# A hybrid streaming encoder: top-k masks taken from ScalarE's signs, and a convolution's input kept as one row

## The chip, the cores and the metric

The kernel runs on 1 core of one Trainium2 chip. The metric is the device time of one execution in microseconds (us); before the change it is 2071.84 us, the median of 3 runs (2068.47 to 2072.87). Engines are named as in the profile: PE (matmul), PEld (its weight loads), DVE (VectorE), ACT (ScalarE), POOL (GpSimd) and SP (which issues the DMAs).

## The reference, cut to what matters

The program is one inference step of a two-layer encoder, for 1024 prompt tokens and 64 sample tokens (1088 in all). Each layer normalises x, projects it with one combined matrix `w_in` to 5204 columns, and feeds three branches: A, a causal convolution of width 4 and a gated linear recurrence; B, sparse attention; C, a causal convolution of width 4, SiLU and a chunked state-space scan (SSD). Their outputs are concatenated, projected by `w_out` and added to x. The parts that the change touches are these:

```python
def causal_conv(x, buf, w, b):              # CONV_WIDTH = 4, buf holds the last 3 tokens
    xp = jnp.concatenate([buf, x], axis=1)
    y = b
    for j in range(CONV_WIDTH):
        y = y + xp[:, j:j + T] * w[j]
    return y, xp[:, T:]

# in sparse_attention, for each block of 64 query tokens
score = sum_h w[t,h] * relu(q_idx[t,h] . k_idx[s])
score = jnp.where(admissible, score, -jnp.inf)
_, idx = lax.top_k(score, k_top)            # k_top = min(256, keys // 4)
# ... attention runs over the chosen keys alone
```

`top_k` takes the highest scores and, among equal ones, those that stand first.

## The kernel before, in words

**Layout.** Channels stand on partitions and tokens along the free axis, in three chunks of 384, 384 and 320 tokens. A projection of one block of 128 columns (`projection`, `three`) takes, for each chunk, 24 matmuls: 8 row tiles of h, three products each (L215 to L217), because both operands are split into a high and a low part. The result lies in one of three PSUM banks named `mm` until ACT or DVE has evacuated it; transposes and small products use two banks named `tp`. A chunk's matmuls therefore wait for the evacuation of the chunk three before.

**Selection.** For seven tiles j of query tokens (score rows `sc` of 384, 512, ... 1024 and 576 keys; six of 128 rows, the last of 64) `select` finds each row's threshold by a binary search over the bits of a float: 31 steps, four tiles counted by ACT with Sign and an accumulator (L580), three by DVE (L574). Before the search the scores are multiplied by a sign `sg` (+1 or -1 per row) so that the threshold sought is never negative (`flip`, L583). After it a mask is made for each tile: the scores are flipped back (L583), DVE counts those at or below the threshold (L574, `le`), marks those equal to it (L631, `eq`), numbers the equal ones by a scan (L634, into `sc`, which is not needed any more), keeps those that stand beyond the number that is wanted (L633, L636, L637), and multiplies by 2^100 (L638). The mask (0 chosen, 2^100 not) goes into `shared`. `select` is a generator: one search step or one mask per `yield`; `pace()` takes one step after each projection, at a lower priority, and what is left runs after `steps(g[0])`.

**Convolution.** `conv_project` projects a block and lets `evac` write each chunk into a tile `raw` of 387 columns: 3 columns of history and 384 of data. The history of chunks 1 and 2 is copied by DVE from the tile of the chunk before (L831); chunk 0's is set to 0 (L833). In chunk 2 the sample's 3 history columns come from the state (L838) between the prompt's and the sample's tokens, and two copies keep the new state (L841, L842). There are 3 buffers of `raw`, one per chunk. `conv4` reads four shifted views of `raw`: one on ACT (L849), with `spare` a second one on ACT and POOL (L852, L853), the others on DVE (L855). Twelve blocks of branch C (`xbc`) run in the stretch of the search, four of branch A (`lru`) after the masks.

**What sets the order.** The order on each engine is fixed when the program is built: a scheduler takes the operations by priority, in about the order of the code, and places them by a simulated timeline; `PLAN` is the list of blocks (`x`, `X` a convolution block of branch C, `z` and `a` gates, `q` a query block, `s` a step of the SSD scan, `l` and `g` branch A). When the chip runs, each engine takes its own instructions strictly in that order. Near the masks stand in the code: the last `x` blocks, then `a0 q1 q0 a1`. A gate (L411 on ACT, L412 on DVE) and a query block (`normed`: transposes L652 on PE, squares L657 on ACT, products L658 on DVE) need DVE to free their PSUM banks.

## Time and profile before

| | |
|---|---|
| median of 3 runs | 2071.84 us |
| profiled execution | 2070.2 us, of which the span from first to last instruction is 2068.4 us |
| PE busy | 1962.7 us (95%) |
| PEld busy | 1755.5 us (85%) |
| DVE busy | 1530.1 us (74%) |
| ACT busy | 1206.6 us (58%) |
| POOL busy | 648.1 us (31%) |
| mean granted TensorE clock | 0.975 |

Read it by stages, not as a whole. Layer 0 fills the time to about 1030 us, layer 1 the rest, with the same stages: normalisation and scores, then (150 to 400 us) projections beside the threshold search, then (400 to 475 us) the masks, then branch A and the second half of SSD (to 675 us), attention and the output projection. An engine that is busy 58% over the span may be idle in the one stage that matters, or bound it. Matmuls are pipelined: their count in a window says more than their busy time. A wait is put down to the instruction that came last.

### The profile page before, as it was taken

The page shows a single profiled execution, that of the slowest core. Times are in us where ns is not written, and L with a number is a line of the kernel's source. Part 1 is how long each engine was busy: PE and PEld are TensorE (multiplying, and loading weights), DVE is VectorE, ACT ScalarE, POOL GpSimd, SP SyncE. Part 2 cuts the span into 40 slices and gives each one's busy share as a digit, 9 for nine tenths or more (in the row PEclk, how much of TensorE's full clock was granted, in tenths as well). Part 3 has the DMA queues.
Part 4 walks back from the last instruction along what each step waited for, and adds up shares of the span by engine and source line. Part 5 has one row for each costly group of instructions (what it writes and reads, how often), then busy time and mean ns, then how long its engine had stood idle before and what let it go on. Part 6 is the DMA issues. An engine that isn't in the chain of part 4 may idle for free.

```text
span 2068.4 us, 34696 instructions
## 1 busy us (share of the span) xinstructions
PE 1962.7 (95%) x12056; PEld 1755.5 (85%) x12056; DVE 1530.1 (74%) x3805; ACT 1206.6 (58%) x2525; POOL 648.1 (31%) x561
## 2 busy tenths in 40 slices
PE   6999999899899899999999999998999998999999
PEld 5899989888789787866998998998888887877689
DVE  7778999997867855564387889999976868456723
ACT  6579898624655544454355798985256655444521
POOL 3012244323522422243430222444243314223320
PEclk9999999999999899999999999999999998999999
DMA  6124354526433632324541433545254246224145
GB/s 225 62 78 135 99 172 130 165 77 164 118 105 108 205 111 87 109 81 128 193 135 38 120 128 105 152 140 162 68 162 113 93 149 194 91 96 141 42 137 173
DMA packets 252080, 257.95 MB, mean 125 GB/s; under 512 B 31264, under 2 KB 230304, under 8 KB 251904
## 3 DMA queue, kind: packets, MB, share of 16 engines
q1 hardware_dynamic: 251904, 255.73, 40.3%
q8 instruction: 95, 1.56, 0.3%
q14 instruction: 81, 0.66, 0.1%
HBM read 181.09 MB, written 74.57 MB: 124 GB/s over the span
## 4 chain that ended last, share of the span: by engine, by line
PE 60%; DVE 20%; DMA 9%; ACT 6%; issue 4%; SPq 1%; POOL 1%; DVEq 0%; ACTq 0%; POOLq 0%
PE mm L215 14%; PE mm L216 14%; PE mm L217 14%; PE s L1098 4%; PE tp L1093 3%; PE s L1068 3%; DMA cumB<-cumd 2%; ACT junka L580 2%; DVE u L855 1%; PE s L881 1%; DVE junk L574 1%; PE s L514 1%; ACT cumB L739 1%; DVE cumB L741 1%; DMA xsc<-xsd 1%
## 5 line engine op out<-in xcount | busy, mean ns | idle before, releaser
L193 POOL TENSOR_TENSOR wlo<-wraw,whi 128x1024 fp32r<-128x1024 f32 x80 | 197.8, 2472 | 361.4 <-ACT whi L192 361.1
L580 ACT ACTIVATE junka<-sc,cand 128x768 bf16<-128x768 f32 x248 | 239.3, 968 | 9.9 <-DVE cand L600 5.7
L192 ACT ACTIVATE whi<-wraw 128x1024 fp32r<-128x1024 f32 x130 | 137.0, 1054 | 136.2 <-PE mm L216 82.6
L1075 ACT ACTIVATE lg<-lg,mx 128x512 f32<-128x512 f32 (+8 forms) x144 | 111.1, 772 | 105.4 <-DVE mx L1071 105.1
L1095 ACT ACTIVATE pT<-tp 128x512 f32<-128x512 f32 (+1 forms) x164 | 90.0, 567 | 114.9 <-PE tp L1093 113.5
L1060 POOL TENSOR_TENSOR nbm<-nb,shared 128x256 f32<-128x256 f32 (+1 forms) x112 | 80.9, 727 | 242.2 <-DVE mx L1071 219.7
L855 DVE SCALAR_TENSOR_TENSOR u<-raw,parh,u 128x384 f32<-128x384 f32 (+1 forms) x198 | 134.7, 689 | 8.9 <-POOL u L853 4.5
L574 DVE TENSOR_SCALAR_CACHE_REDUCE junk<-sc,cand 128x384 bf16<-128x384 f32 (+4 forms) x194 | 140.0, 753 | 0.9
L1068 PE MATMUL s<-kst,qst 128*128 128x512 f32 (+4 forms) x448 | 119.3, 363 | 10.5 <-DVE mx L1071 10.5
L739 ACT ACTIVATE cumB<-cumB,ctk 128x128 f32<-128x128 f32 (+1 forms) x288 | 88.4, 384 | 51.4 <-DMA cumB<-cumd 51.1
L1093 PEld LDWEIGHTS tp<-identr,lg 128*128 128x128 f32 (+2 forms) x656 | 71.5, 140 | 48.7 <-issue 42.2
L1093 PE MATMUL tp<-identr,lg 128*128 128x128 f32 (+2 forms) x656 | 108.5, 278 | 0.5 <-DVE lg L1078 0.5
L1098 PE MATMUL s<-pT,vt 128*64 128x256 f32 (+2 forms) x656 | 106.8, 391 | 1.6 <-ACT pT L1095 1.6
L215 PE MATMUL mm<-sth0a,whi 128*128 128x384 f32 (+1 forms) x228 | 84.2, 370 | 16.9 <-DVE g L412 11.2
L1071 DVE CUSTOM_DVE_ANT_0 lg<-s,shared 128x512 f32<-128x512 f32 (+4 forms) x112 | 61.5, 553 | 46.7 <-PE s L1068 41.7
L1068 PEld LDWEIGHTS s<-kst,qst 128*128 128x128 f32 (+1 forms) x448 | 72.3, 188 | 25.4 <-DVE mx L1071 16.7
L1078 DVE TENSOR_SCALAR lg<-lg,ri 128x512 f32<-128x512 f32 (+8 forms) x144 | 87.1, 607 | 3.2
L1143 DVE TENSOR_TENSOR xl<-xl,mm 128x384 f32<-128x384 f32 (+1 forms) x40 | 21.4, 540 | 90.1 <-PE mm L217 71.3
L216 PE MATMUL mm<-stl0a,whi 128*128 128x384 f32 (+1 forms) x228 | 80.0, 351 | 2.1 <-POOL stl0a L954 1.6
L193 DVE TENSOR_TENSOR wlo<-wraw,whi 128x1024 fp32r<-128x1024 f32 x50 | 63.6, 1271 | 23.9 <-ACT whi L192 23.6
L216 PE MATMUL mm<-stl1a,whi 128*128 128x384 f32 (+1 forms) x228 | 80.2, 352 | 1.0 <-DVE stl1a L954 0.8
L217 PE MATMUL mm<-sth3a,wlo 128*128 128x384 f32 (+1 forms) x228 | 80.5, 353 | 0.0
(474 smaller groups left out, 6915.9 us busy)
## 6 DMA issues: line engine op xcount, KB each, us to landing
wraw<-in_w_in_dram SPq DMA_DIRECT2D x82, 512.0 KB, 3.4
wraw<-in_w_out_dram SPq DMA_DIRECT2D x48, 512.0 KB, 3.8
cumB<-cumd SPq DMA_DIRECT2D x32, 512.0 KB, 5.2
xsd<-u SPq DMA_DIRECT2D x48, 192.0 KB, 2.3
gz<-gzd SPq DMA_DIRECT2D x32, 256.0 KB, 3.7
xsc<-xsd SPq DMA_DIRECT2D x32, 256.0 KB, 3.7
eB<-cumd SPq DMA_DIRECT2D x56, 128.0 KB, 3.7
gzd<-g SPq DMA_DIRECT2D x32, 192.0 KB, 1.9
```

The lines of the kernel that those rows point to most:

```text
L192: S.activation(hi, raw, AF.Copy)
L193: eng.tensor_tensor(lo, raw, hi.bitcast(F32), op=OP.subtract)
L215: PE.matmul(ps, hi[:, k, :], xh[ci][:, c0:], start=k == 0, stop=False)
L216: PE.matmul(ps, hi[:, k, :], xl[ci][:, c0:], start=False, stop=False)
L217: PE.matmul(ps, lo[:, k, :], xh[ci][:, c0:], start=False, stop=k == len(xs) - 1)
L574: V.tensor_scalar(junk, sc[j][:n], thr, None, op0=op, op1=OP.add, accum_out=out)
L580: S.activation(junk, sc[j][:n], AF.Sign, scale=-1.0, bias=cand, accum_out=out)
L855: V.scalar_tensor_tensor(u, raw[:, j:j + n], w[:, wbase + j * wstride:wbase + j * wstride + 1], u, op0=OP.mult, op1=OP.add)
L1068: PE.matmul(ps[:nq, :b - a], qst[:, h, :nq], kst[:, g, pt, kbase + a:kbase + b], start=pt == 0, stop=pt == 1)
L1075: S.activation(lg[:nq, :nk], lg[:nq, :nk], AF.Exp, scale=-1.0, bias=mx[:nq, h, k_ - 1:k_], accum_out=sm[:nq, h:h + 1])
L1093: PE.transpose(ps[:n, i * nq:(i + 1) * nq], lgs[h][:nq, j * 128:j * 128 + n], ident[:nq, :nq])
L1098: PE.matmul(av[64 * b:64 * b + 64, :, :nq], vt[:n, vj, 64 * g:64 * g + 64], pT[:n, 2 * b:2 * b + 2, :nq], start=j == 0, stop=j == nb_ - 1)
```

## The change

The masks: the flip back and DVE's count are gone. ACT writes Sign(threshold - score) into a tile `junka` for each score row (its scale is -`sg`, so the flipped scores serve as they are), with the row's sum of signs in `cnt`; the tile holds -1, 0 or 1. DVE finds the equal ones by comparing `junka` with 0, scans them as before, works out `need` from the sum of signs and from the scan's last column (two instructions instead of one), and joins the equal ones that are not chosen by a max in place of the subtraction. ACT makes the mask: Relu with scale 2^100. The two buffers of `junka` are those that the search used.

The convolution: `raw` is one row of 1030 columns for a whole block, in 2 buffers instead of 3 of a chunk each. Each chunk is evacuated to its place in that row, so the two copies of history (L831) go; the memset and the copy of the sample's history stand at the block's start.

```diff
--- before.py
+++ after.py
@@ -20,7 +20,7 @@
 
 DEPTH = 2
 PLAN = ('', 'X8 x10 z2 x1 x0 z3 x2 x3 s0 x9 s0 z4 s0 x11 s0 z5 s0 z6 s0 x4 s0 X5 s0 z7 s0 s0 X6 x7', 's0 s1 a0 q1 s0 q0 s1 a1', 's1 s1 q3 q2 s1 l0 s1 g0 s1 l1 g1 s1 s1 l2 g2 s1 l3 s1 g3', 'a3 a2')
-RAW = 3
+RAW = 2
 U1 = 1
 HG = ((0, 2, 4, 5, 6), (3, 5, 7))
 KV = 1
@@ -621,21 +621,24 @@
                 count(j, col("cand", j).bitcast(F32), col("cnt", j), OP.is_ge)
             V.tensor_tensor(keep, f["cnt"][:, 3:], f["kq"][:, 3:], op=OP.is_ge)
             V.copy_predicated(M, keep, cand)
+
             V.tensor_tensor(f["thr"], f["M"].bitcast(F32), f["sg"], op=OP.mult)
+            V.tensor_scalar(f["sg"], f["sg"], -1.0, None, op0=OP.mult)
             for j in range(7):
                 n = part(j)
-                thr = col("thr", j)
-                flip(j)
-                le = count(j, thr, col("cnt", j), OP.is_le)
+                junk = scp.tile([128, 1024], BF, name="junka", bufs=2)[:n, :nks[j]]
+                S.activation(junk, sc[j][:n], AF.Sign, scale=col("sg", j), bias=col("thr", j), accum_out=col("cnt", j))
                 eq = scp.tile([128, 1024], BF, name="junk", bufs=2)[:n, :nks[j]]
-                V.tensor_scalar(eq, sc[j][:n], thr, None, op0=OP.is_equal)
-                need = small.tile([128, 1], F32, name="need")
-                V.tensor_scalar(need[:n], col("cnt", j), 1.0, float(kk[j] - nks[j]), op0=OP.mult, op1=OP.add)
+                V.tensor_scalar(eq, junk, 0.0, None, op0=OP.is_equal)
                 V.tensor_tensor_scan(sc[j][:n], ones[:n, 0:1].to_broadcast([n, nks[j]]), eq, 0.0,
                                      op0=OP.mult, op1=OP.add)
-                V.scalar_tensor_tensor(eq, sc[j][:n], need[:n], eq, op0=OP.is_le, op1=OP.mult)
-                V.tensor_tensor(le, le, eq, op=OP.subtract)
-                V.tensor_scalar(mask[j][:n], le, BIG, None, op0=OP.mult)
+
+                need = small.tile([128, 1], F32, name="need")
+                V.tensor_tensor(need[:n], col("cnt", j), sc[j][:n, nks[j] - 1:nks[j]], op=OP.add)
+                V.tensor_scalar(need[:n], need[:n], 0.5, float(kk[j] - nks[j] / 2), op0=OP.mult, op1=OP.add)
+                V.scalar_tensor_tensor(eq, sc[j][:n], need[:n], eq, op0=OP.is_gt, op1=OP.mult)
+                V.tensor_tensor(junk, junk, eq, op=OP.max)
+                S.activation(mask[j][:n], junk, AF.Relu, scale=BIG)
                 yield
 
 
@@ -822,25 +825,22 @@
         def conv_project(pl, off, state0, nt, t, c0, use):
 
 
-            rows = []
+            raw = pl.tile([128, RW], F32, name="raw", bufs=RAW)
+            V.memset(raw[:, 0:3], 0.0)
+            V.tensor_copy(raw[:, TP + 3:TP + 6], par[:, state0 + t:state0 + t + 2 * nt + 1:nt])
+            at = [0]
 
             def evac(a, b, ps):
-                ci = len(rows)
-                raw = pl.tile([128, 387], F32, name="raw", bufs=RAW)
-                if ci:
-                    V.tensor_copy(raw[:, 0:3], rows[-1][:, 384:387])
+                ci = at[0]
+                at[0] += 1
+                if ci < 2:
+                    S.activation(raw[:, a + 3:b + 3], ps[:, :b - a], AF.Copy)
                 else:
-                    V.memset(raw[:, 0:3], 0.0)
-                rows.append(raw)
-                if ci < 2:
-                    S.activation(raw[:, 3:387], ps[:, :384], AF.Copy)
-                else:
-                    V.tensor_copy(raw[:, 259:262], par[:, state0 + t:state0 + t + 2 * nt + 1:nt])
-                    S.activation(raw[:, 3:259], ps[:, :256], AF.Copy)
-                    S.activation(raw[:, 262:326], ps[:, 256:320], AF.Copy)
-                    V.tensor_copy(stc[:, c0 + t:c0 + t + 2 * nt + 1:nt], raw[:, 256:259])
-                    V.tensor_copy(stc[:, c0 + 3 * nt + t:c0 + 5 * nt + t + 1:nt], raw[:, 323:326])
-                use(raw, ci)
+                    S.activation(raw[:, a + 3:TP + 3], ps[:, :TP - a], AF.Copy)
+                    S.activation(raw[:, TP + 6:RW], ps[:, TP - a:b - a], AF.Copy)
+                    V.tensor_copy(stc[:, c0 + t:c0 + t + 2 * nt + 1:nt], raw[:, TP:TP + 3])
+                    V.tensor_copy(stc[:, c0 + 3 * nt + t:c0 + 5 * nt + t + 1:nt], raw[:, RW - 3:RW])
+                use(raw[:, PCH[ci][0]:], ci)
             project(off + 128 * t, evac)
 
         def conv4(pl, raw, u, w, wbase, wstride, bias, spare):
```

Some lines get other numbers: the scan L634 is L633 after the change, L652 is L655, L658 is L661, L731 is L734, L741 is L744; L412 and L855 keep theirs.

DVE in layer 0, up to the evacuation of the first chunk of gate a0 (`g`, L412); `sc_638` is the score tile of 384 keys, `u` the convolution, `cumB`, `eB`, `yC`, `cbm` belong to the SSD scan. Before:

```order
L855 SCALAR_TENSOR_TENSOR u<-raw,parh,u 128x384
L791 TENSOR_TENSOR eB<-eB,s_4693 128x512
L574 TENSOR_SCALAR junk,cnt<-sc_638,thr 128x384
L631 TENSOR_SCALAR junk<-sc_638,thr 128x384
L741 TENSOR_TENSOR cumB<-cumB,cbm 128x1024
L865 SCALAR_TENSOR_TENSOR u<-th,u 128x384
L792 TENSOR_TENSOR yC<-xsc,eB 128x4x128
L633 TENSOR_SCALAR need<-cnt 128x1
L634 SCALAR_TENSOR_TENSOR sc_638<-ones,junk 128x384
L865 SCALAR_TENSOR_TENSOR u<-th,u 128x384
L855 SCALAR_TENSOR_TENSOR u<-raw,parh,u 128x323
L412 SCALAR_TENSOR_TENSOR g_4834<-g_4834,mm 128x384
```

After:

```order
L574 TENSOR_SCALAR junk,cnt<-sc_643,cand 128x1024
L841 COPY stc<-raw 128x3
L842 COPY stc<-raw 128x3
L865 SCALAR_TENSOR_TENSOR u<-th,u 128x323
L725 TENSOR_TENSOR cbm<-tp,triu 128x128
L574 TENSOR_SCALAR junk,cnt<-sc_644,cand 64x576
L855 SCALAR_TENSOR_TENSOR u<-raw,parh,u 128x384 x2
L794 TENSOR_TENSOR eB<-eB,s_4645 128x512
L744 TENSOR_TENSOR cumB<-cumB,cbm 128x1024
L622 TENSOR_TENSOR keep<-cnt,kq 128x4
L855 SCALAR_TENSOR_TENSOR u<-raw,parh,u 128x384
L412 SCALAR_TENSOR_TENSOR g_4786<-g_4786,mm 128x384
```

Before, the count, the comparison and the scan of the first mask stood ahead of that evacuation; after, the masks have not begun there, and what stands ahead belongs to the last counts of the search, the convolution and the scan. The flips of the four long tiles, which stood 15 to 25 rows higher, are gone.

DVE in layer 0, one mask after the other; `need` and `cnt` are columns of one number per row. Before, the second mask, without its last row (the multiplication L638):

```order
L574 TENSOR_SCALAR junk,cnt<-sc_639,thr 128x512
L631 TENSOR_SCALAR junk<-sc_639,thr 128x512
L633 TENSOR_SCALAR need<-cnt 128x1
L634 SCALAR_TENSOR_TENSOR sc_639<-ones,junk 128x512
L412 SCALAR_TENSOR_TENSOR g_4892<-g_4892,mm 128x320
L865 SCALAR_TENSOR_TENSOR u<-th,u 128x323
L636 SCALAR_TENSOR_TENSOR junk<-sc_639,need,junk 128x512
L731 TENSOR_TENSOR xdt<-tp,dt 128x512
L722 TENSOR_TENSOR cbm<-tp,triu 128x128
L637 TENSOR_TENSOR junk<-junk 128x512
L741 TENSOR_TENSOR cumB<-cumB,cbm 128x1024
L646 MEMSET qt 64x128 x2
```

After, the first and second masks, without the second's last row (its max):

```order
L632 TENSOR_SCALAR junk<-junka 128x384
L633 SCALAR_TENSOR_TENSOR sc_638<-ones,junk 128x384
L632 TENSOR_SCALAR junk<-junka 128x512
L637 TENSOR_TENSOR need<-cnt,sc_638 128x1
L633 SCALAR_TENSOR_TENSOR sc_639<-ones,junk 128x512
L638 TENSOR_SCALAR need<-need 128x1
L649 MEMSET qt 64x128 x2
L637 TENSOR_TENSOR need<-cnt,sc_639 128x1
L639 SCALAR_TENSOR_TENSOR junk<-sc_638,need,junk 128x384
L638 TENSOR_SCALAR need<-need 128x1
L640 TENSOR_TENSOR junka<-junka,junk 128x384
L639 SCALAR_TENSOR_TENSOR junk<-sc_639,need,junk 128x512
```

After, two masks run interleaved, as there are two buffers of `junka`; the count, the subtraction and the multiplication are not among DVE's rows.

ACT in layer 0 at the same place; `cmB` is the row of query block q1 on its way out of an `mm` bank, `bt` and `cumB` belong to the scan, `whi` is the split of a weight block. Before:

```order
L411 ACTIVATE g_4892<-mm 128x320
L864 ACTIVATE th<-u 128x323
L724 ACTIVATE bt<-tp 128x128
L395 ACTIVATE cmB<-mm 128x384 x2
L739 ACTIVATE cumB<-cumB,ctk 128x128 x8
L192 ACTIVATE whi<-wraw 128x1024
L395 ACTIVATE cmB<-mm 128x320
L657 ACTIVATE g_5023<-tp 128x384
L740 ACTIVATE cumB<-cumB 128x1024
```

After:

```order
L630 ACTIVATE junka,cnt<-sc_638,thr,sg 128x384
L630 ACTIVATE junka,cnt<-sc_639,thr,sg 128x512
L395 ACTIVATE cmB<-mm 128x384
L641 ACTIVATE shared<-junka 128x384
L630 ACTIVATE junka,cnt<-sc_640,thr,sg 128x640
L727 ACTIVATE bt<-tp 128x128
L641 ACTIVATE shared<-junka 128x512
L395 ACTIVATE cmB<-mm 128x384
L630 ACTIVATE junka,cnt<-sc_641,thr,sg 128x768
L192 ACTIVATE whi<-wraw 128x1024
L395 ACTIVATE cmB<-mm 128x320
L641 ACTIVATE shared<-junka 128x640
```

ACT takes on the signs (L630) and the masks (L641) between the evacuations of q1's three chunks; each L641 waits for DVE's max of that tile, and the L630 two tiles on waits for it in turn.

## Rows read from the trace of the kernel before

**Rows 1.** Page, section 1: busy us (share of the span) and instructions.

```profile
PE 1962.7 (95%) x12056; PEld 1755.5 (85%) x12056; DVE 1530.1 (74%) x3805; ACT 1206.6 (58%) x2525; POOL 648.1 (31%) x561
```

**Rows 2.** Windows by stage: PE, PEld, DVE, ACT, POOL busy (instructions), PE clock, DMA share, GB/s.

```profile
150.00:400.00 250.00, 246.62 (x1580) 236.39 (x1579) 231.95 (x575) 221.24 (x488) 92.52 (x68) 1.00 0.49 144
400.00:475.00 75.00, 65.23 (x393) 61.67 (x393) 74.50 (x159) 22.89 (x55) 18.10 (x12) 0.93 0.30 93
475.00:675.00 200.00, 187.90 (x1137) 171.20 (x1135) 144.92 (x287) 113.02 (x209) 66.39 (x55) 0.97 0.42 121
1425.00:1500.00 75.00, 65.98 (x382) 62.70 (x381) 74.59 (x160) 24.44 (x57) 18.71 (x11) 0.91 0.29 92
```

**Rows 3.** Waits of PE, whole span: us in total, times, longest us.

```profile
PE tp L728 <- DMA xsc<-xsd: 16.3, 9, 3.0
...
PE mm L215 <- DVE g L412: 11.2, 3, 5.7
...
PE tp L652 <- DVE qt L658: 7.2, 2, 3.7
```

**Rows 4.** Timeline of PE: start us, us, instruction [idle before it, releaser].

```profile
413.01 0.69 PE L215 MATMUL mm<-sth0a,whi 128*128 128x384 f32 x1 [5.68 <-DVE g L412]
...
442.58 0.52 PE L652 MATMUL tp<-identr,cmB 128*128 128x128 f32 x3 [3.67 <-DVE qt L658]
...
1439.84 0.69 PE L215 MATMUL mm<-sth0a,whi 128*128 128x384 f32 x1 [5.35 <-DVE g L412]
...
1469.25 0.88 PE L652 MATMUL tp<-identr,cmB 128*128 128x128 f32 x3 [3.52 <-DVE qt L658]
```

**Rows 5.** Windows just after the restart at 413.01, same columns as the stages.

```profile
414.00:416.00 2.00, 2.00 (x8) 2.00 (x7) 2.00 (x7) 1.37 (x3) 0.14 (x1) 0.50 0.85 216
416.00:418.00 2.00, 2.00 (x14) 1.98 (x14) 2.00 (x5) 1.41 (x3) 1.92 (x3) 0.86 1.02 311
```

**Rows 6.** Timeline of DVE ahead of the late gate evacuation, layer 0.

```profile
397.06 0.67 DVE L583 TENSOR_SCALAR sc<-sc,sg 128x896 f32<-128x896 f32 x1
...
407.50 0.60 DVE L574 TENSOR_SCALAR_CACHE_REDUCE junk<-sc,thr 128x384 bf16<-128x384 f32 x1
...
410.64 0.94 DVE L634 TENSOR_TENSOR_SCAN sc<-ones,junk 128x384 f32<-128x384 f32 x1
...
412.42 0.54 DVE L412 SCALAR_TENSOR_TENSOR g<-g,mm 128x384 f32<-128x384 f32 x1
```

**Rows 7.** Groups by line, DVE, both layers: count, busy us, mean ns, idle before.

```profile
L634 DVE TENSOR_TENSOR_SCAN sc<-ones,junk 128x384 f32<-128x384 f32 (+6 forms) x14 | 22.4, 1596 | 0.0
...
L583 DVE TENSOR_SCALAR sc<-sc,sg 128x384 f32<-128x384 f32 (+6 forms) x28 | 14.9, 568 | 0.0
...
L831 DVE COPY raw<-raw 128x3 f32<-128x3 f32 x64 | 13.3, 208 | 11.0 <-ACT raw L836 10.8
...
L574 DVE TENSOR_SCALAR_CACHE_REDUCE junk<-sc,thr 128x384 bf16<-128x384 f32 (+6 forms) x14 | 12.8, 914 | 0.0
...
L631 DVE TENSOR_SCALAR junk<-sc,thr 128x384 bf16<-128x384 f32 (+6 forms) x14 | 10.5, 748 | 0.0
...
L638 DVE TENSOR_SCALAR shared<-junk 128x384 bf16<-128x384 bf16 (+6 forms) x14 | 6.5, 464 | 0.1
...
L633 DVE TENSOR_SCALAR need<-cnt 128x1 f32<-128x1 f32 (+1 forms) x14 | 1.9, 137 | 0.0
```

**Rows 8.** Groups by line and shape, ACT.

```profile
L580 ACT ACTIVATE junka<-sc,cand 128x768 bf16<-128x768 f32 x62 | 57.7, 930 | 9.9 <-DVE cand L600 5.7 <-DVE sc L583 3.6 <-DVE rs_tg L160 0.6
...
L580 ACT ACTIVATION_READ_ACCUMULATOR junka<-sc,cand 128x1 f32 x186 | 35.7, 192 | 0.0
...
L1075 ACT ACTIVATE lg<-lg,mx 128x384 f32<-128x384 f32 x16 | 9.7, 610 | 5.0 <-DVE mx L1071 4.6
```

**Rows 9.** Chain that ended last, 465 to 690 us: start us, us, what.

```profile
479.42 2.13 DVE yC L792
481.56 4.18 DMA xsc<-xsd
```

## The prediction

> **What bounds the kernel now.** I read the shares first: PE is busy 95% of the span, DVE 74%, ACT 58% [rows 1]. By that PE bounds everything, so the next view is the table by stages [rows 2]. From 150 to 400 us PE starts 1580 matmuls in 250 us at full clock, one in 158 ns, and shows 246.6 us busy: work taken from another engine buys nothing there. From 400 to 475 us, where the masks are made, it is the other way round. DVE is busy 74.5 of 75 us, PE 65.2, with 393 matmuls at a mean clock of 0.93; layer 1 has the same picture at 1425 us (74.6 and 66.0, clock 0.91). From 475 to 675 us neither is full: PE 187.9 of 200, DVE 144.9.
>
> Third, the waits of PE [rows 3]. Two kinds point at DVE as the late one: a projection that waits for a bank that the gate's evacuation L412 holds (11.2 us) and q1's transposes that wait for L658 (7.2 us). The timeline has them: 5.68 and 3.67 us in layer 0, 5.35 and 3.52 us in layer 1, 18.2 us, all inside the two mask stages [rows 4]. Each has a tail. When PE restarts at 413.01 us it runs at half clock, 0.50 from 414 to 416 and 0.86 from 416 to 418 us, 8 matmuls in the first window and 14 in the second [rows 5]. A mean of 0.86 over 2 us means half clock until 416.56, so 3.55 us at half speed, a loss of 1.8 us. I give each of the four stalls that tail: 7.2 us. The ceiling of what the mask stages can return is then 18.2 + 7.2 = 25.4 us, 12.7 a layer.
>
> Why DVE is late is seen in its own timeline [rows 6]: it has no gap, and ahead of the evacuation at 412.42 us stand flips (397.06), a count (407.50) and a scan (410.64).
>
> **The change part by part.** DVE, both layers together [rows 7]:
> - The flips back are half of the 28 of L583: 14.9 / 2 = 7.5 us gone.
> - The 14 counts, 12.8 us gone.
> - The 14 multiplications by 2^100, 6.5 us gone, to ACT.
> - The comparison now reads bf16 instead of f32. The nearest row for one input and an output of bf16 is L638, 6.5 us for the same shapes against 10.5 us of L631: 4.0 us gone. Bounds: 0 (as slow as now) to 4.0.
> - `need` takes a second instruction, 14 times, and `sg` is negated twice: 16 x 137 ns of L633 = 2.2 us more.
> - The max stands where the subtraction stood, same operands: nothing.
>
> Sum 7.5 + 12.8 + 6.5 + 4.0 - 2.2 = 28.6 us, 14.3 a layer. The 64 copies of history take 13.3 us. 48 of them belong to blocks of branch C, nearly all of which run before 400 us, where PE hides them: nothing, beyond DVE coming to the masks with a shorter queue. 16 belong to branch A, 16 x 208 ns = 3.3 us, in a stage where DVE has 55 of 200 us idle: 0 to 3.3, and I take 1, as idle DVE is nearer to hiding them.
>
> Where this lies: DVE's 74.5 us of a mask stage become 74.5 - 14.3 = 60.2. PE, without stalls and tails, needs 75 - 12.7 = 62.3. So the bound passes back to PE, but by 2 us only, and the two engines lean on each other through the banks. I don't expect the whole ceiling. The first stall should go: in the new order the masks have not begun when the gate's first chunk is evacuated, so the count and scan of [rows 6] stand behind it, and the flips are gone. The second may stay in part: q1's and q0's evacuations stand between masks in the new order too, so a mask round still delays them.
>
> The change adds waits. ACT's relu of a tile waits for DVE's max; behind it in ACT's queue stand evacuations of q1 and the sign of the tile two on, since there are two buffers; DVE's comparison waits for that sign. A sign costs what L580 does, 930 ns for 768 keys and 192 ns for its sum [rows 8]. Seven tiles make four rounds of two; a round that nothing covers costs DVE 1.1 us, four of them 4.4 us a layer. Bounds 0 (the order puts work of the scan between the rounds) to 4.4. I take 4.4, because ACT's queue also has other work before each sign: 12.7 - 4.4 = 8.3 a layer, 16.6 in both.
>
> ACT itself: 14 signs of about 930 + 192 ns and 14 relus between 610 ns (an ACT pass over 384 columns) and 930 [rows 8], so 24 to 29 us more, some 13 a layer. It is busy 22.9 of the 75 us, and goes to 36 of some 66: hidden. Without that cover it would cost its 13 us a layer, which is the slower rival below.
>
> Sum against the profiled execution: 2070.2 (span 2068.4 plus 1.8 around it) - 16.6 - 1 = 2052.6. The median of the runs shown is 1.6 us above that execution, less than I can resolve; I say 2053.
>
> **The rivals.**
>
> *Slower: ACT's queue holds the banks.* The place is ACT between 400 and 475 us. Each of the seven relus stands in front of an evacuation, and if the relu comes early in the queue it waits for what is left of DVE's mask: a scan and what follows it, 1.6 us and 1 us more (the scan is 1596 ns [rows 7]; for the rest I take two instructions of some 500 to 700 ns, as L638 and L631 there). Seven times 2.6 us is 18 us a layer. The three banks absorb 2 chunks of 24 matmuls of 158 ns, 7.6 us. The other 10.6 us stall PE, 21 us in both layers, while at least half of the old stalls goes, 13 us: +8, so 2078 us. It decides from the point where ACT's waits for L640 pass 7.6 + 12.7, some 20 us a layer. For it speaks that every engine takes its queue in order, and that the relus stand among q1's evacuations; against it that ACT has 52 of 75 us idle and that in the new order a relu follows the max by several instructions. The Trainium skill speaks for it (ScalarE: Activation LUTs, Rules for kernel authors): relu, max and mul belong on VectorE, which is up to about three times faster per element in bf16. The trace agrees on the rate, 464 ns of L638 against 610 ns and more on ACT [rows 7, 8]. By that rule the multiplication is better left where it was, 6.5 us of DVE against some 11 of ACT, and the sum would lose 6.5 instead of gaining it: 2053 + 6.5 + 4.5 = 2064 if both engines stood on the path.
>
> *Given back later.* The order of PE, DVE and SP changes as far as branch A. From 475 us the chain goes over transfers: yC L792 on DVE, then 4.18 us of a DMA that PE's transposes wait for [rows 9], and PE's largest wait of all is for that transfer, 16.3 us [rows 3]. If these transfers have their own pace, the time saved at 475 us is waited for at 480. For it: PE is idle 12 of 200 us there. Against it: the transfer starts when yC L792 ends, so a DVE that is ahead starts it earlier. It leaves a quarter to nothing of the 17.6 us: 2066 to 2072, at the middle 2069.
>
> *Nearly all of it, and more.* The rounds are covered, both stalls go with their tails, the 3.3 us of branch A count, and the new order does a little better in the idle 12 us a layer after the masks: 2070.2 - 25.4 - 3.3 = 2041.5, and to 2036 at the lowest.
>
> *The row is no row.* If a chunk's evacuation into the shared `raw` had to wait for the reads of the chunk before, conv4's four passes would stand between two evacuations. The code reads columns that the evacuation before has written and none that the next one writes, so I give it no chance of its own beyond the slower one.
>
> **How the numbers follow.** Chances: the forecast (2046 to 2060) 0.52; nearly all 0.18; given back 0.18; slower 0.12. What a measurement of this kernel can tell from no change is about 0.2%, 4.1 us: 2067.7 to 2076. The forecast and nearly all lie below it, and of the 0.18 given back I put 0.07 below: faster 0.77. The rest of that case is the same, 0.11; slower 0.12. The range reaches from the lowest of the third rival, 2036, to 2069, which takes in most of what is given back and leaves the slower one out.
>
> **What would show it.** Right: PE's waits for L412 and for L658 (L661 after) fall from 18.4 us to under 7; no window after the first gate at 0.50; the mask stages end 8 to 9 us earlier in each layer; DVE's busy time falls by about 42 us (28.6 + 13.3) and ACT's grows by 24 to 29. The first step is wrong if DVE stays full to the end of the masks and the stalls stay; the covered ACT is wrong if PE or DVE wait for L630, L641 or for evacuations of ACT behind them; the last step is wrong if the masks end early and PE's waits for transfers grow by as much. A stage from 150 to 400 us that got shorter would show that PE was not its bound, and the copies would then be worth what I put at nothing.

## The result and the profile after

The changed kernel took 2046.83 us beside 2070.79 us (medians of four runs each), ratio 0.9884 (95% interval 0.9865 to 0.9904). Beside the later experiments it took 2054.35 us against 2072.37, ratio 0.9916 (0.9890 to 0.9942). So it is 18 to 24 us faster; forecast were 2053 us and a gain of 17.6. Its profiled execution took 2043.88 us with a span of 2042.1.

The shares, as [rows 1]: busy us (share), instructions.

```profile
PE 1952.6 (96%) x12056; PEld 1747.9 (86%) x12056; DVE 1519.2 (74%) x3701; ACT 1231.8 (60%) x2567; POOL 651.2 (32%) x561
```

ACT grew by 25.2 us, as worked out. DVE fell by 10.9 only, not by 42. The stages, as [rows 2] (layer 1's masks 13.5 us earlier, as layer 1 starts earlier):

```profile
150.00:400.00 250.00, 243.19 (x1557) 232.17 (x1557) 226.02 (x537) 219.62 (x487) 90.62 (x68) 1.00 0.49 143
400.00:475.00 75.00, 68.61 (x420) 63.16 (x419) 73.60 (x157) 39.65 (x87) 23.73 (x17) 0.98 0.42 120
475.00:675.00 200.00, 190.85 (x1148) 174.55 (x1146) 145.00 (x279) 109.95 (x201) 66.08 (x51) 0.97 0.39 119
1411.50:1486.50 75.00, 69.29 (x440) 65.00 (x437) 73.68 (x154) 40.52 (x89) 23.29 (x15) 0.98 0.42 125
```

In the 75 us of the masks PE starts 420 matmuls instead of 393 at a clock of 0.98 instead of 0.93; DVE is nearly as full as it was. But in the stage before it starts 23 fewer (1557 against 1580), so from 150 to 475 us it is only four matmuls ahead: not all of the 27 are time won. PE's waits over the span, as [rows 3]:

```profile
PE tp L731 <- DMA xsc<-xsd: 6.8, 6, 2.4
PE tp L655 <- DVE need L637: 5.4, 2, 2.7
...
PE tp L731 <- DVE xdt L734: 2.8, 2, 1.5
...
PE tp L655 <- DVE qt L661: 1.9, 2, 0.9
...
PE mm L215 <- DVE g L412: 1.0, 2, 0.8
```

The two waits of [rows 3] that point at DVE fell from 18.4 to 2.9 us; 5.4 us came back in the same place under another name: q1's transposes still wait for DVE. The waits for the transfer `xsc` fell too, from 16.3 to 6.8 us. The first mask stage in PE's timeline, as [rows 4], and its clock, as [rows 5]:

```profile
416.80 0.65 PE L731 MATMUL tp<-identr,xsc 128*128 128x128 f32 x4 [0.17 <-DMA xsc<-xsd]
...
423.56 0.66 PE L731 MATMUL tp<-identr,xsc 128*128 128x128 f32 x4 [1.49 <-DVE xdt L734]
...
431.48 0.52 PE L655 MATMUL tp<-identr,cmB 128*128 128x128 f32 x3 [2.68 <-DVE need L637]
```

```profile
414.00:416.00 2.00, 2.00 (x14) 2.00 (x13) 2.00 (x2) 0.78 (x3) 2.00 (x2) 1.00 0.85 227
...
434.00:436.00 2.00, 2.00 (x8) 2.00 (x8) 2.00 (x4) 2.00 (x7) 2.00 (x2) 0.50 0.00 0
```

The stall of 5.68 us and its tail are gone; one of 2.68 us, with a tail at half clock, is left. DVE shows why, as [rows 6]:

```profile
407.89 0.56 DVE L412 SCALAR_TENSOR_TENSOR g<-g,mm 128x384 f32<-128x384 f32 x1
...
410.93 0.55 DVE L412 SCALAR_TENSOR_TENSOR g<-g,mm 128x384 f32<-128x384 f32 x1
...
412.47 0.16 DVE L625 TENSOR_TENSOR thr<-M,sg 128x7 f32<-128x7 f32 x1
...
417.50 0.96 DVE L633 TENSOR_TENSOR_SCAN sc<-ones,junk 128x384 f32<-128x384 f32 x1
```

Two evacuations of the gate now come before the threshold (412.47; before, at 406.1), and so before every mask. DVE's and ACT's groups, as [rows 7, 8]:

```profile
L855 DVE SCALAR_TENSOR_TENSOR u<-raw,parh,u 128x384 f32<-128x384 f32 (+1 forms) x198 | 147.4, 751 | 11.7 <-POOL u L853 5.9 <-ACT u L849 4.2
...
L640 DVE TENSOR_TENSOR junka<-junka,junk 128x384 bf16<-128x384 bf16 (+6 forms) x14 | 13.3, 951 | 0.0
...
L583 DVE TENSOR_SCALAR sc<-sc,sg 128x384 f32<-128x384 f32 (+6 forms) x14 | 7.1, 571 | 0.0
L632 DVE TENSOR_SCALAR junk<-junka 128x384 bf16<-128x384 bf16 (+6 forms) x14 | 6.1, 438 | 0.0
```

```profile
L630 ACT ACTIVATE junka<-sc,thr,sg 128x384 bf16<-128x384 f32 (+6 forms) x14 | 13.3, 952 | 0.4
L641 ACT ACTIVATE shared<-junka 128x384 bf16<-128x384 bf16 (+6 forms) x14 | 10.8, 771 | 20.3 <-DVE junka L640 20.3
```

**Where the time went.** From windows of 1 us over the span: PE's idle time, and its time lost at half clock (busy time times one minus the granted clock).

| execution | span | idle | lost at half clock | rest |
|---|---|---|---|---|
| before | 2068.4 | 105.7 | 41.9 | 1920.9 |
| changed, first | 2042.1 | 89.5 | 30.6 | 1922.0 |
| changed, again | 2056.3 | 96.9 | 36.9 | 1922.5 |

The rest, PE's work at full clock, is the same; the gain is gaps and clock. Two executions of the same changed kernel differ by 14 us, so a single trace tells no stage to better than some us. By place, from the starts of two lines of the kernel before (in each layer the last row of L343 to the last of L999, with search, masks and branch A, called the mask half; and from there to the next layer's first L343 or the end, with attention and the output projection), both layers added; below the first row, differences from it:

| execution | mask half | attention half |
|---|---|---|
| before | 1319.5 | 670.2 |
| changed, first / again | -14.0 / -8.3 | -11.6 / -7.0 |
| masks alone | -1.2 | +0.7 |
| row alone | -1.9 | -7.2 |
| passes added back to DVE | -10.0 | -5.7 |
| relu on DVE | -18.7 | -7.1 |
| search early, changed kernel's work | +18.2 | -5.9 |
| all copies added back | 0.0 | -6.0 |
| copies in branch A / in branch C | -9.4 / -6.2 | -8.7 / -0.8 |

I had placed all of the gain in the first column.

**Gaps and clock, over all executions.** A trace is one execution, but every execution has its span and its mean granted clock on record. Span times clock is an estimate of what the span would be at full clock; the rest of the span is lost to the clock (here half of any idle time at half clock is in it too). Means in us, with standard errors of 0.5 to 1.4 and 0.7 to 1.9; one slow execution of the kernel before, of 10505.6 us, is left out:

| kernel | executions | at full clock | lost to the clock |
|---|---|---|---|
| before | 72 | 2024.4 | 44.9 |
| changed | 10 | 2012.9 | 36.9 |
| masks alone | 12 | 2020.6 | 48.3 |
| row alone | 12 | 2013.2 | 45.5 |
| passes added back to DVE | 9 | 2020.6 | 34.7 |
| relu on DVE | 6 | 2017.9 | 27.6 |
| masks, late search | 12 | 2025.7 | 39.6 |
| before, late search | 12 | 2026.3 | 36.8 |
| all copies added back | 12 | 2023.3 | 43.9 |
| search early, changed kernel's work | 12 | 2036.7 | 39.8 |
| copies in branch A | 6 | 2016.7 | 32.8 |
| copies in branch C | 7 | 2025.5 | 30.9 |
| search later still, changed kernel's work | 6 | 2017.2 | 38.4 |

The row alone has the whole gain at full clock, 11.2 us, and nothing of the clock. The masks on top of it add nothing at full clock and 8.6 us of clock. One execution can't tell this: single ones scatter by 2 to 5 us in the first column, and the two profiled ones of before and of the row alone show it the other way round (2016.7 and 2018.3 at full clock).

### The profile page after: what moved, and what is told of

The parts are those of the page before. It is cut to its first block, busy times and chain, and to the rows that moved or that the text cites. A ratio compares the mean times of both kernels' runs of the same rounds, so it can differ in the third digit from the quotient of the medians.

```text
span 2042.1 us, 34620 instructions
## 1 busy us (share of the span) xinstructions
PE 1952.6 (96%) x12056; PEld 1747.9 (86%) x12056; DVE 1519.2 (74%) x3701; ACT 1231.8 (60%) x2567; POOL 651.2 (32%) x561
## 4 chain that ended last, share of the span: by engine, by line
PE 66%; DVE 19%; DMA 6%; ACT 5%; issue 3%; SPq 1%; POOL 0%; DVEq 0%; ACTq 0%
PE mm L216 16%; PE mm L215 15%; PE mm L217 15%; PE s L1098 4%; PE tp L1093 4%; PE s L1068 3%; DVE u L855 2%; ACT junka L580 2%; PE s L881 1%; DMA cumB<-cumd 1%; PE s L514 1%; DMA eB<-cumd 1%; ACT cumB L742 1%; DMA xsc<-xsd 1%; PE s L791 1%
## 5 line engine op out<-in xcount | busy, mean ns | idle before, releaser
L855 DVE SCALAR_TENSOR_TENSOR u<-raw,parh,u 128x384 f32<-128x384 f32 (+1 forms) x198 | 147.4, 751 | 11.7 <-POOL u L853 5.9
L1068 PE MATMUL s<-kst,qst 128*128 128x512 f32 (+4 forms) x448 | 120.8, 362 | 7.8 <-DVE mx L1071 7.3
L1078 DVE TENSOR_SCALAR lg<-lg,ri 128x512 f32<-128x512 f32 (+8 forms) x144 | 93.6, 651 | 3.3
L1068 PEld LDWEIGHTS s<-kst,qst 128*128 128x128 f32 (+1 forms) x448 | 72.2, 188 | 21.9 <-DVE mx L1071 13.4
L778 POOL TENSOR_TENSOR hT<-hT,dec 128x512 f32<-128x512 f32 x28 | 35.9, 1282 | 144.3 <-DVE hT L780 137.0
```

Source lines behind the costliest of these rows:

```text
L855: V.scalar_tensor_tensor(u, raw[:, j:j + n], w[:, wbase + j * wstride:wbase + j * wstride + 1], u, op0=OP.mult, op1=OP.add)
L1068: PE.matmul(ps[:nq, :b - a], qst[:, h, :nq], kst[:, g, pt, kbase + a:kbase + b], start=pt == 0, stop=pt == 1)
```

## The experiments

Ratios are to the kernel before, with their 95% intervals.

**Masks alone.** The diff's lines up to L641; `RAW` and `conv_project` as before.

> The kernel before with the masks of the change alone; the convolution keeps its three chunk tiles and its 64 copies of history. Bookkeeping of PE (span = idle + time lost at half clock + the rest) gives the change 26.3 us in the profiled executions: 9.7 in the two mask stages (400 to 470 and 1425 to 1495 us of before), 9.2 in the last stretch of the two attention stages (883 to 960.6 and 1903.9 to 1981.2 us), 4.3 between, the rest small. Theory A (two separate gains: the masks give the mask stages, and the attention's end is a matter of the order there, which in this kernel is that of before): 2071 - 10 to 14 = 2057 to 2061, and PE waits again near 891 us for L1071's maximum with half clock behind it. Theory B (one gain: what the masks save makes the attention's loads come at a better time, the copies are worth nothing): 2046 to 2050, without that stall. Theory C (the copies in the way of the masks are what mattered): 2066 to 2071.

Measured: 2069.66 us, ratio 1.0009 (0.9988 to 1.0030): nothing. DVE is relieved as worked out (busy 1500.7 us, 29.4 less), and in the masks it has gaps, yet PE starts fewer matmuls than before. Windows, then PE's timeline in both layers, then ACT's and DVE's:

```profile
400.00:475.00 75.00, 61.84 (x372) 58.04 (x370) 70.26 (x155) 33.70 (x74) 23.42 (x16) 0.91 0.41 117
```

```profile
407.95 0.31 PE L217 MATMUL mm<-sth3b,wlo 128*128 128x320 f32 x1
417.70 1.11 PE L731 MATMUL tp<-identr,xsc 128*128 128x128 f32 x4 [9.44 <-DMA xsc<-xsd]
...
419.10 0.61 PE L215 MATMUL mm<-sth4b,whi 128*128 128x320 f32 x1
...
1442.40 1.12 PE L731 MATMUL tp<-identr,xsc 128*128 128x128 f32 x4 [7.02 <-DMA xsc<-xsd]
```

```profile
412.03 2.45 ACT L742 ACTIVATE cumB<-cumB,ctk 128x128 f32<-128x128 f32 x8 [4.30 <-DMA cumB<-cumd]
414.38 0.47 ACT L411 ACTIVATE g<-mm 128x384 f32<-128x384 f32 x1
```

```profile
414.88 0.56 DVE L412 SCALAR_TENSOR_TENSOR g<-g,mm 128x384 f32<-128x384 f32 x1 [0.88 <-ACT g L411]
```

PE stops in the middle of a chunk (after `sth3b`; `sth4b` comes at 419.10), because transposes that wait for a transfer stand there in its queue. The gate's evacuation is no earlier than it was, at 414.88, but it isn't DVE that holds it: DVE waits 0.88 us for ACT's half of the gate (L411), which stands in ACT's queue behind a step of the scan that waited 4.30 us for a DMA. What was a wait for L412 is now a longer one for `xsc`. Theory A's and B's times are missed; the time fits C, and the copies below refute C as an account of their duration.

**Row alone.** The diff's other lines.

> The kernel before with the convolution's row alone; flips, counts and the multiplication by 2^100 stay on DVE. The order of PE differs from before's by little up to the masks, and above all in the attention stage (slices 12 to 17 of 40 of its rows). Theory A (the attention's end is a matter of the order, and that comes with the row): 9 to 12 us faster, 2059 to 2062, the stall at 891 us shorter or gone, and the mask stages as before (PE waits of 5 us for L412 and 3.5 us for L658 in each). Theory B (all from the masks): 2067 to 2073, no difference that can be told. My prediction's step for the copies (1, at most 3.3 us): 2067 to 2070.

Measured: 2060.14 us, ratio 0.9957 (0.9935 to 0.9979), as theory A. My step for the copies forecast 1 us. PE in the first mask stage:

```profile
411.91 0.45 PE L215 MATMUL mm<-sth0a,whi 128*128 128x384 f32 x1 [0.29 <-DVE g L412]
...
433.41 0.55 PE L652 MATMUL tp<-identr,cmB 128*128 128x128 f32 x3 [3.28 <-DVE xdt L731]
...
481.88 1.98 PE L788 MATMUL s<-cumB,xdt 128*64 128x128 f32 x16 [4.31 <-DVE xdt L731]
```

Contrary to what theory A said of the masks, the stall at the gate is gone in layer 0 without any change to them: the row brings the order in which the gate comes before the threshold (417.8 us here). In layer 1 DVE has the same order, and theory A is right: 4.68 us of the stall are left. PE, then DVE:

```profile
1434.65 0.69 PE L215 MATMUL mm<-sth0a,whi 128*128 128x384 f32 x1 [4.68 <-DVE g L412]
```

```profile
1431.40 2.30 DVE L622 TENSOR_TENSOR keep<-cnt,kq 128x4 int32<-128x4 f32 x1
```

Ahead of that evacuation stand the four long flips, 2.5 us, which the masks' half of the change removes, and this comparison of four columns, which lasts 2.30 us beside a pass of POOL and 0.15 us in layer 0. The later stalls, behind full-length masks, stay. The attention half is 7.2 us shorter.

**Passes added back to DVE.** In the changed kernel, ahead of each sign:

```diff
+V.tensor_scalar(sc[j][:n], sc[j][:n], 1.0, None, op0=OP.mult)
+count(j, col("thr", j), spare, OP.is_le)
```

> The changed kernel with the removed passes back as work that decides nothing: ahead of each tile's sign DVE multiplies the scores by one in place (as the flip did) and counts them into a spare column (as the count did): 28 instructions, 20.3 us of DVE over both layers by the durations of before (7.5 of flips and 12.8 of counts). Theory A (DVE's length in the mask stage is what the masks gain): the 9.7 us of the mask stages go again, 2055 to 2060, DVE still full there and PE waiting for it 8 us or more a layer. Rival (the gain comes from the order and from ACT, not from DVE's passes): within 3 us of 2047.

Measured: 2057.18 us, ratio 0.9942 (0.9921 to 0.9963). Against the changed kernel's two ratios that is 0.26 to 0.58%, 5 to 12 us. Beside 0.9916 the intervals overlap, so the lower end is not resolved. Its mask stage kept its matmuls, with DVE full:

```profile
400.00:475.00 75.00, 70.22 (x429) 66.49 (x425) 74.32 (x171) 36.52 (x79) 19.36 (x12) 0.98 0.34 103
```

So theory A's place is wrong even if its time is met: 20.3 us of DVE passes cost 5 to 12, and not by emptying PE there.

**The relu on DVE.**

```diff
-S.activation(mask[j][:n], junk, AF.Relu, scale=BIG)
+V.tensor_scalar(mask[j][:n], junk, 0.0, BIG, op0=OP.max, op1=OP.mult)
```

> The changed kernel with the last step of each mask on DVE: one instruction (maximum with 0, times 2^100) takes the place of ACT's relu. By L638 of before that is 6.5 us of DVE over both layers, and 10.8 us of ACT's L641 and its 20 us of waiting for L640 go. Theory A (DVE bounds the mask stage): slower by 3 to 7 us, 2050 to 2054. Rival, that of my prediction (ACT's relu in its queue holds the evacuations behind it): faster by 2 to 6, 2041 to 2045. If the two cancel: 2045 to 2049.

Measured: 2047.52 us, ratio 0.9902 (0.9875 to 0.9929): the same as the changed kernel. ACT's waits between 398 and 480 us, in the changed kernel and here:

```profile
ACT shared L641 <- DVE junka L640: 10.0, 5, 4.0
```

```profile
ACT junka L630 <- DVE shared L641: 15.9, 5, 5.4
```

ACT's sign waits for DVE instead of its relu, and PE gains nothing by either. Where the multiplication stands decides nothing here, and the rule that the prediction took from the Trainium skill (ScalarE: Activation LUTs, Rules for kernel authors), which puts it on VectorE, neither costs nor gains a measurable time.

**Masks with a late search.** The masks alone, and one number:

```diff
-LATE = 100
+LATE = 500
```

> The masks of the change alone, chunk tiles and copies as before, and one number changed: LATE, the priority by which the scheduler puts the search's steps behind, is 500 instead of 100. With it the threshold stands on DVE behind the first evacuations of gate a0, as in the changed kernel; with 100 (the run of the masks alone) it stood ahead of them, and PE then waited 9.4 and 7.0 us in one piece for DMA xsc. Theory D (the row's worth is the order in front of the masks, and without it what the masks save turns into that wait): 2046 to 2055, PE's longest wait between 400 and 480 us under 4 us. Rival (the row's worth is DVE time, 13.3 us of copies, or its storage): 2063 to 2071, as the masks alone.

Measured: 2066.57 us, ratio 0.9984 (0.9964 to 1.0005): not theory D's. In the profiled execution, the fastest of the twelve at 2055.13 us, the stalls are as D said (longest 2.06 us, for L412; `xsc` 8.5 us in all, against 29.5 with the masks alone). But PE's idle time over its span is 105.2 us, as before (105.7): what is saved at the gate is waited for elsewhere, and this execution is fast by its clock (21.3 us lost at half clock, against 41.9). To have the gate first is not enough.

**The kernel before with a late search.** The same number, nothing else.

> The kernel before with LATE 500 instead of 100 and nothing else: the threshold stands on DVE behind three evacuations of the gate, the work is that of before. Theory D (order): what the row alone gave, 2057 to 2064, without the 5.7 us wait for L412. Rival (copies or storage): 2067 to 2073. Between this run and the masks with LATE 500 lies the worth of the masks in the late order: 8 to 12 us by theory D.

Measured: 2064.31 us, ratio 0.9965 (0.9947 to 0.9984): the order alone, with all of the old work, gives 7 us, at the edge of theory D's range. But it isn't the row's gain by another way. PE's waits for L412 stay, if shorter, where D expected the 5.7 us to be gone:

```profile
415.68 0.69 PE L215 MATMUL mm<-sth0a,whi 128*128 128x384 f32 x1 [3.00 <-DVE g L412]
...
1439.02 0.69 PE L215 MATMUL mm<-sth0a,whi 128*128 128x384 f32 x1 [4.74 <-DVE g L412]
```

And by the table of gaps and clock this gain is all clock (36.8 against 44.9 us lost), while the row's is all at full clock. The masks in this order (the run above) are worth nothing, where D said 8 to 12.

**All copies added back.** In the changed kernel:

```diff
+if ci:
+    V.tensor_copy(pl.tile([128, 3], F32, name="hist", bufs=2), raw[:, a:a + 3])
```

> The changed kernel with 64 copies of three columns added where the copies of history stood (into a spare tile; nothing reads it): 13.3 us of DVE by L831 of before. The order up to the masks stays that of the changed kernel on PE. Theory D (the copies' time is worth nothing, PE hides it): 2043 to 2051. Rival (the copies' time is what the row saves): 2053 to 2060.

Measured: 2067.47 us, ratio 0.9990 (0.9968 to 1.0011). Both are wrong: the loss, 0.74 to 1.06% or 15 to 22 us, is more than the 13.3 us that the copies last. DVE's busy time grows by 4.5 us only (1523.7 against 1519.2). Up to 415 us PE keeps the changed kernel's order; from there on it has another.

**Search early.** The changed kernel with `LATE = -2000`.

> The changed kernel with LATE -2000: the search's steps are put in front, and the threshold stands on DVE ahead of the gate's first evacuation and of six passes of the convolution, as in the masks alone. All the work is that of the changed kernel. Theory D (order): the gain is mostly lost, 2060 to 2071, and a long wait of PE (5 us or more) shows up between 400 and 420 us. Rival (DVE's time is what counts, wherever the masks stand): 2044 to 2052.

Measured: 2077.50 us, ratio 1.0022 (0.9999 to 1.0044): all of the gain is lost, with the changed kernel's work, and more than theory D said. DVE, then PE, then PE's waits over the span:

```profile
416.43 0.15 DVE L625 TENSOR_TENSOR thr<-M,sg 128x7 f32<-128x7 f32 x1
420.32 0.54 DVE L412 SCALAR_TENSOR_TENSOR g<-g,mm 128x384 f32<-128x384 f32 x1
```

```profile
426.12 1.11 PE L731 MATMUL tp<-identr,xsc 128*128 128x128 f32 x4 [6.45 <-DMA xsc<-xsd]
```

```profile
PE tp L731 <- DMA xsc<-xsd: 29.1, 14, 6.4
```

The picture of the masks alone: threshold before gate, and waits for `xsc` of 29.1 us against 6.8 (10.2 in the changed kernel's second execution). The loss is in gaps: 2036.7 us at full clock against 2012.9.

**The changed kernel again.**

> The changed kernel once more, unaltered, beside the three runs that vary it, since only four times of it are known (2043.9 to 2050.0). Expected 2044 to 2052. Bookkeeping by the mean granted clock: of the 24 us that it is faster, some 12 are PE idle (time less span times one minus clock) and some 10 the clock (0.983 against 0.978). If the attention's end was an accident of the profiled execution, this execution shows the stall of about 3 us before L1068 in one of the layers again.

Measured: 2054.35 us, ratio 0.9916 (0.9890 to 0.9942), a little over the times expected. Its stall before L1068 in layer 1, and a window of 2 us that begins some 6 us after PE's restart:

```profile
1901.41 0.56 PE L1068 MATMUL s<-kst,qst 128*64 128x384 f32 x2 [2.44 <-DVE mx L1071]
```

```profile
1907.00:1909.00 2.00, 2.00 (x8) 1.45 (x7) 1.28 (x4) 0.82 (x3) 0.42 (x1) 0.50 0.24 67
```

The same two in the first execution:

```profile
1892.02 0.57 PE L1068 MATMUL s<-kst,qst 128*64 128x384 f32 x2 [2.46 <-DVE mx L1071]
```

```profile
1898.00:1900.00 2.00, 2.00 (x15) 1.75 (x13) 1.62 (x6) 0.03 (x1) 0.20 (x1) 1.00 0.50 131
```

In the windows between the clock is 0.50 from 1903 us on in the one execution and 1.00 in the other: the same stall was followed by half clock once, and once not.

**Copies in branch A alone, and in branch C alone.** The lines of the copies above under `if ci and pl is not cv`, and under `if ci and pl is cv`.

> The changed kernel with copies of three columns into a spare tile in branch A alone: 16 instructions, 3.3 us of DVE by L831 of before. The order of every engine stays that of the changed kernel but for 22 rows of PE and 20 of DVE, so this prices the copies without the order. My prediction's step: 1 us, 0 to 3.3, so 2045 to 2051. Rival (the copies stand in front of a convolution that PE waits for, and the 20 us that all 64 cost in the run before come from here): 2056 to 2066.

Measured: 2052.05 us, ratio 0.9899 (0.9874 to 0.9924): no cost that can be told from the changed kernel beside it (2054.35), with the order held; both lie a little over the range. The step (1 us) holds.

> The changed kernel with the same copies in branch C alone: 48 instructions, 10.0 us of DVE, most of them before 400 us. Here the order changes from the masks on (4103 of 9896 rows of PE). My prediction's step: nothing, 2044 to 2051. Rival E (a few hundred ns of DVE per block are enough for the scheduler to place the work after the masks in another order, and that order costs more than the copies): 2056 to 2068, with the loss behind 470 us, not in 150 to 400 us.

Measured: 2059.08 us, ratio 0.9936 (0.9909 to 0.9963), 5 us over the changed kernel beside it, intervals overlapping: outside my step's range and inside rival E's. Branch A's copies cost nothing and branch C's about 5 where all together cost 15 to 22: as times, the prices don't add up. By the table of gaps and clock most of that is the clock. At full clock branch C's copies cost 12.6 us, all together 10.4 and branch A's 3.8; branch C's lost less to the clock (30.9 us) and all together more (43.9). Branch A's keep the changed kernel's order; in the other two PE's order changes from 416 us on, so this isn't a price of the copies alone.

**Search later still.** The changed kernel with `LATE = 500`.

> The changed kernel with LATE 500: same work, the threshold on DVE behind three evacuations of gate a0 instead of two, and another order from there on. With LATE -2000 the same work took 2077.5. Theory D (what matters is that the gate's evacuations come before the masks): 2042 to 2052. Rival E (every new order of the same work scatters by some 10 us, whatever stands first): anywhere from 2045 to 2068, and outside 2042 to 2052 would speak for it.

Measured: 2058.64 us, ratio 0.9926 (0.9897 to 0.9955), 4 us over the changed kernel beside it, not resolved. This run and the changed kernel beside it both lie outside theory D's range, so the run doesn't decide.

No run beat the changed kernel by more than the measurement.

## Why the prediction was right, step by step

**The sum** was right: 17.6 us forecast, 18 to 24 measured. Its division was not: 16.6 for the masks and 1 for the row, where the masks alone give nothing, the row alone 9, and both 18 to 24. That the terms add up to about the time measured is luck: neither holds by itself, and nearly half of the gain lies in the attention half, which I had put at nothing.

**The row: the step that failed** is "48 belong to blocks of branch C [...]: nothing, beyond DVE coming to the masks with a shorter queue". For branch A's 16 copies, with the order held, the 1 us stands. As the price of the row it failed: the row gives 9 us of time, 11.2 at full clock, and branch C's copies, put back, cost 12.6 of that. The row changes what the scheduler puts before what, and so did each of these runs but branch A's. That another order moves as much without a copy less is shown by the kernel before (7 us, by the clock) and, the other way, by the search early.

**The first stall** went for the reason given, masks that have not begun at the gate's first evacuation. But I booked that order to the masks; by the two halves it comes with the row, and the masks alone keep the old one. It needs both halves: with the row alone, its flips still ahead of the gate, 4.68 us of the stall are left in layer 1; with both, no wait for L412 is over 0.8 us.

**The masks** are worth 8 to 15 us on top of the row (0.9884 and 0.9916 against 0.9957; with 0.9916 the intervals overlap), near the 16.6, and nothing without it. But by the averages they are worth it in clock, 8.6 us, where at least 9.4 us of my 16.6 were stalls (16.6 less the 7.2 of the tails). Putting the flips and counts back costs 5 to 12 of it.

**DVE's relief** of 28.6 us was right in size (29.4 with the masks alone). The copies' 13.3 us were not: they are a sum of durations, and the next instruction starts before a copy ends, 0.08 us after its start in the median of the 64. Before the change:

```profile
381.74 0.16 DVE L831 COPY raw<-raw 128x3 f32<-128x3 f32 x1
381.81 0.67 DVE L791 TENSOR_TENSOR eB<-eB,s 128x512 f32<-128x512 f32 x1
```

Without the 64 copies DVE's busy time before would be 4.6 us shorter, no more. So some 34 us should have gone, and 10.9 went, since other passes of DVE then last longer: L855, untouched, takes 134.7 us before, 125.8 with the masks alone (there L858) and 147.4 in the changed kernel. An example, POOL's and then DVE's timeline in the changed kernel:

```profile
434.31 3.11 POOL L193 TENSOR_TENSOR wlo<-wraw,whi 128x1024 fp32r<-128x1024 f32 x1
```

```profile
435.22 2.61 DVE L640 TENSOR_TENSOR junka<-junka,junk 128x768 bf16<-128x768 bf16 x1
...
447.19 0.61 DVE L640 TENSOR_TENSOR junka<-junka,junk 128x896 bf16<-128x896 bf16 x1
```

The first L640 ends 0.4 us after POOL's pass; the second, for more keys and with POOL idle, takes 0.61 us. Over the span I added up what each DVE instruction lasted beyond the lower quartile of its group (same line, tiles and shape), where that is over 0.15 us: 167 us before, 183 after, 183 again, 160 with the masks alone, and beside all of it POOL was busy for a part of the instruction at least. The Trainium skill (GPSIMD Engine Reference, 1. Specifications) says that POOL and VectorE share SBUF interfaces and contend where the DVE instruction has two SBUF inputs or runs in a performance mode of two ports; L640, with two inputs, agrees.

**The uncovered rounds** (4.4 us a layer) cost nothing: DVE's only wait between 398 and 480 us is 0.3 us, and not for the signs. That DVE's 74.5 us of a mask stage become 60.2 failed: in the same window it is busy 73.6 us.

**The tails**, 1.8 us for each of four stalls, were too regular: lost at half clock were 41.9 us before, 30.6 and 36.9 after, so 5 to 11 us returned where 7.2 were counted, and part of it in the attention half.

**Signs.** "Under 7 us" for the waits for L412 and L661 is met by name (2.9), but not with the 5.4 us that the same transposes wait for `need`. "Mask stages 8 to 9 us earlier" failed. The last mask of layer 0, before and after:

```profile
472.35 0.29 DVE L638 TENSOR_SCALAR shared<-junk 64x576 bf16<-64x576 bf16 x1
```

```profile
469.91 0.67 ACT L641 ACTIVATE shared<-junka 64x576 bf16<-64x576 bf16 x1
```

It ends 2.1 us earlier; in layer 1 15.1, of which that layer starts 13.6 earlier. The blocks q3 and q2 behind the masks gain 5.0 and 5.7 us (the start of the last L661 before attention; in layer 1 from its last L343). Another 7.0 to 11.6 us came from the attention half, of which I had forecast nothing; the row alone has 7.2 of it and the masks alone none.

**Rivals.** The slower one did not come: ACT's waits for L640 are 10 us a layer, under its point of 20. "Given back later" is what the masks alone do, not at 480 us but at 417, inside the masks.

**What stays open.** Why the masks with a late search and chunk tiles stay at 2066.6, which part of the order behind the masks carries the 15 to 22 us of the copies, and why some orders lose less to the clock. The search early shows that order alone can take all of the gain away. That the row's gain is its order, and not its storage or its missing copies, is not shown: a version with the changed kernel's order and the old tiles wasn't made.

## What to carry to other kernels

Where a scheduler fixes each engine's order from a model, price a change twice: once by the instructions that it removes, and once by the new order, read beforehand at the places where the busiest engine waits. Look there for what stands in front of a freed bank, and for instructions that wait for a transfer in the middle of work that is ready. Test the halves of a change apart, and run one control in which only the order moves. Compare such runs at full clock (span times granted clock, over all executions) as well as by time: here two runs with a like gain in time had it from different sources.

## What the runs showed of the hardware

- One kernel's times scatter with the clock, in part. In twelve executions of the masks alone times from 2061.57 us (mean granted clock 0.980) to 2080.46 (0.973) have a standard deviation of 5.3 us; less the span times one minus the clock, of 1.8. For the 25 executions of the kernel before beside them it is 5.0 and 4.2, so there most of the scatter is not the clock's.
- A stall of 2.4 us before the same matmul was followed by a granted clock of 0.50 in one execution and of 1.00 in another.
- Beside a pass of POOL a DVE pass over 768 columns lasted 2.61 us, where 896 columns take 0.61 us alone; one over 4 columns lasted 2.30 us, where it takes 0.15 us elsewhere.
- A DVE copy of 3 columns lasts 0.16 us, but the next instruction starts 0.07 us after it does.
